# Two-operand arithmetic of the S5 and GLA stages on VectorE alone, table copies on ScalarE, other task lengths in the order

## The chip, the cores and the metric

One core of a Trainium2 chip runs the whole program. TensorE (PE in the rows) multiplies matrices, VectorE (DVE) and ScalarE (ACT) work on elements, GpSimd (POOL) does too and issues some DMAs, SyncE (SP) issues most DMAs. The metric is the device time of one execution in microseconds (us); lower is better.

## The reference

One layer of a hybrid model on 640 tokens (512 latent, 128 context) of 1024 features, in float32. What is computed, cut to what matters here:

```python
h = rms_norm(x) * (1 + scale1) + shift1
q, k, v, r, glr, u, ga, gb = split(h @ w_in)
# GLA: 4 heads, 2 directions, chunks of 64 tokens
log_a = log_sigmoid(glr @ w_gate_up + b_gate) / 16
cum = cumsum(log_a, within a chunk)
q_dec, k_in, k_out = q*exp(cum), k*exp(-cum), k*exp(total-cum)
o = tril(q_dec @ k_in.T) @ v + q_dec @ state;  state = exp(total)*state + k_out.T @ v
o_gla = rms_norm(o) * silu(r)
# S5: 32 groups of 16 channels, 64 complex states a group, 2 directions
lam_bar = exp(lam * exp(log_step)); b_bar = (lam_bar-1)/lam * b
s[t] = lam_bar * s[t-1] + b_bar @ u[t];  y = Re(c @ s) + d*u
o_s5 = gelu(y) * sigmoid(gelu(y) @ w_glu + b_glu)
merged = sigmoid(ga)*(o_gla @ w_proj_gla) + sigmoid(gb)*(o_s5 @ w_proj_s5)
x = x + gate1 * (merged @ w_out)
x = x + gate2 * (relu((rms_norm(x)*(1+scale2)+shift2) @ w_ff1)**2 @ w_ff2)
```

## The kernel before

**The main stream.** The weights come as slabs of 128x1024 through SyncE's queue (line 150). Each slab is split into two parts of lower precision: ScalarE rounds the high part `whi` (line 167), VectorE subtracts for the low part `wlo` (line 174). The features are split likewise into `hh` and `hl`, so that every product is three TensorE products of 320 or 512 columns (`whi`hh, `whi`hl, `wlo`hh). There are two buffers each of `whi` and `wlo`: a slab is split while the one before it is multiplied. The products come in units of one slab: u (4 units), k and q (4 each), v (8), then the S5 gate GLU, the low-rank gate, the S5 projection `ps`, the gates r and gb (8 units each), `gp` (the GLA projection, which merges), `wo`, and the two feed-forward products.

**The side work.** S5 and GLA run beside this stream. Each piece is a task: an engine, an estimated length, a function. The class `Sides` is a list scheduler that runs while the program is written: it counts up a planned time by the products that it has emitted, and emits a task between two products once the estimates say that its inputs are there. So the lengths decide at which place in every engine's list of instructions a task stands; on the chip each engine works through its own list in that order and waits by semaphore where an input isn't there yet. `sd.force()` at the end of v and at the end of gb emits all tasks that are left, with no products between them.

**S5's tasks**, for four sets q of eight channel groups (called group 0 to 3 below) and two directions d: `G` builds the input kernel from powers of lambda (two 128x1152 multiplications and an addition: `s5_g1` to `s5_g3`), `T` transposes it (line 844), `C` builds the output kernel in the same way (`s5_c1` to `s5_c3`), `K` multiplies both (32 products) and `P` stores the result to DRAM and reads it back as a Toeplitz matrix, `U` and `V` bring in u (which goes through DRAM too), `B` makes the rotation tables (`s5_tab`: six 128x256 operations and three copies), `R` rotates, scans and rotates back on VectorE (scans on lines 966 and 968), `Y` and `O` give the output, GELU on ScalarE follows. `C` of a group may not start before `Y` of the group before has read the old result, and `B` needs `R` of the group before. Before all of them stand constants that depend on lambda alone: `lam_p` on GpSimd makes the powers for the tables, `lt`, `lx`, `lq0` and `lq1` those for G and C.

**GLA's tasks**, for four heads: `z` (gate, logarithm, running sum, exponentials), `qk0` to `qk2` (decayed q and k), `kt` (transposes of k), `sm` and `st` (states), `sc` (scores), `fin`, `oa` to `oc` (outputs), `no` (norm), `og` (transposes and the gate r). A gate unit (r, gb) is followed by a logistic function in four steps on ScalarE and VectorE and a multiplication.

**The helpers.** `tt(o, a, b, op, e)` (line 207) is a two-operand operation on VectorE, or on GpSimd where the last argument is `G`; `mm` (line 219) is a product. Nearly all rows of the trace therefore have one of these two lines, and the tile names and shapes tell them apart. Names: `B`, `H` and `XB` are the working tiles, `aux` the single PSUM banks of the side work, `mm` the banks of the stream, `raw` the loaded slabs. In this version GpSimd has one of the two multiplications of each `G` and `C`, the six operations of every `B`, half of the lambda powers (`lq0`), `qk2` and the last multiplication after each r unit.

Of the kernel before, what the change touches and what calls it, by code (L numbers as in the profile page):

```python
# [29 lines left out]
class Sides:  # L30
    """Static list scheduler. The main stream of matrix products is emitted in order; the side work is a list of
    tasks with estimated lengths per engine, each emitted between the products when its inputs should be there."""
# [10 lines left out]
    def add(self, name, steps, after=(), banks=0, at=0.0, first=False, lazy=False):  # L43
        """a chain of steps (engine, length, function); the chain ends with the name given."""
        new = []
        for n, (eng, us, fn) in enumerate(steps):
            last = n == len(steps) - 1
            new.append((name if last else f"{name}.{n}", eng, us, fn, tuple(after), banks, at))
            after, banks, at = [f"{name}.{n}"], 0, 0.0
            if lazy:  # L50
                self.lazy.add(new[-1][0])
        if first:
            n = max((j + 1 for j, t in enumerate(self.todo) if t[0][:1] == "w" and name[0] == "w"), default=0)
            self.todo[n:n] = new
        else:
            self.todo += new
# [55 lines left out]
    def chain(self, name, wait=True):  # L112
        """emits what is left of a chain and lets the main stream wait for its end."""
        self.finish(*[t[0] for t in self.todo if t[0] == name or t[0].startswith(name + ".")])
        if wait:
            self.now["PE"] = max(self.now["PE"], self.end[name])

    def room(self, banks):
        """lets the side work go on until banks are free."""
        while 4 - len(self.held) < banks:  # L120
            self.run(next(t for t in self.todo if t[5] <= 4 - len(self.held) and all(a in self.end for a in t[4])))

    def force(self, name=None):
        """emits everything up to a task, whatever the estimates say."""
        while self.todo and (name is None or any(t[0] == name for t in self.todo)):
            self.run(self.todo[0])


class Weights:
    """Streams the weight slabs: DMA ahead, then an exact split into two float32r parts."""  # L130
# [24 lines left out]
    def ahead(self, w):  # L155
        """plans the splits of the main stream's slabs up to the w-th."""
# [24 lines left out]
    def first(self):  # L181
        """the first slab's raw data and the tiles of its parts, which the caller splits."""
        hi, lo = (self.pool.tile([128, 1024], F32R, tag=t, name=t, bufs=2) for t in ("whi", "wlo"))
        self.cut, self.parts[0], raw = 1, (hi, lo), self.raw.pop(0)
        self.sides.end["w0"] = 0.0
        self.top_up()
        return hi, lo, raw
# [14 lines left out]
def hybrid(tc, A, O):  # L202
# [19 lines left out]
    with contextlib.ExitStack() as ctx:  # L222
# [29 lines left out]
        # ---------------------------------------------------------------- first loads  # L252
# [66 lines left out]
        # ---------------------------------------------------------------- startup  # L319
# [33 lines left out]
        # ---- S5 constants that depend on lambda only, on the pair columns  # L353
        def sgt(o, a, s, b, op0, op1, tmp):
            """(a op0 s) op1 b on Pool, which has no single instruction for it."""
            ts(tmp, a, s, op0, e=G)
            tt(o, tmp, b, op1, G)
# [76 lines left out]
        def lam_5():  # L434
            # coefficient (lambda_bar - 1) / lambda
            ts(t2, LR, -1.0, ADD)
            tt(CR, t2, lre, MUL)
            tt(va, LI, lim, MUL)
            tt(CR, CR, va, ADD)
            tt(CR, CR, den, MUL)  # L440
# [8 lines left out]
        def lam_6():  # L449
            # ... times the conjugate of the phase of lambda^8  # L450
# [12 lines left out]
        def lam_p():  # L463
            # powers of the phase of lambda^8
# [26 lines left out]
        # stacked powers: X = [re; im] of lambda^k, Y = i * X, per group  # L491
# [47 lines left out]
        # ---- adaLN  # L539
# [5 lines left out]
        def mod_first(bank, j, i, a=None):  # L545
            """shift1 and scale1 of 256 features: even contraction tiles in the first two row groups, odd ones in the others."""
# [33 lines left out]
        # ---- position embedding and the first norm's statistics  # L580
# [41 lines left out]
        def warm(n):  # L622
            """keeps the tensor engine's clock up while the first data arrives."""
# [77 lines left out]
        def tok_unit(w, hi, lo, kts, banks, first, last, hooks={}, ahead=1, order=range(5)):  # L701
            """token-major: rows of 128 tokens times 512 columns, two contraction tiles."""
# [18 lines left out]
        def feat_part(ps, parts, hi, lo, first, n, nk=8, sub=0, lead=None):  # L721
            """feature-major: 128 features times n tokens."""
# [49 lines left out]
        # ---------------------------------------------------------------- S5  # L772
# [21 lines left out]
        S5 = {}  # L794
# [14 lines left out]
        def s5_g1(q, d):  # L809
            Bv, bb, kv = s5_views(q, d)  # L810
            tt(prod, bb(Bv[1]), kv(Q2, d), MUL, G)
# [10 lines left out]
        def s5_c1(q, d):  # L822
            Bv, bb, kv = s5_views(q, d)
            tt(prod, bb(Bv[3]), kv(YY, d), MUL, G)
# [59 lines left out]
        def s5_tab(q, d):  # L884
# [7 lines left out]
            tt(vr_, ar, br, MUL, G)  # L892
            tt(w, ai, bi, MUL, G)
            tt(vr_, vr_, w, SUB, G)
            tt(vi_, ar, bi, MUL, G)
            tt(w, ai, br, MUL, G)
            tt(vi_, vi_, w, ADD, G)
            for tab in (tabr, tabi):
                G.tensor_copy(tab[:, d, :, 64:80], tab[:, d, :, 48 * d:48 * d + 16])
            G.tensor_copy(rho_t[:, d], rho[:, cols][:, :, None].to_broadcast([128, 4, 81]))  # L900
# [35 lines left out]
        def s5_r1(q, d):  # L936
            """rotates the chunk inputs and sets the starting states."""
# [36 lines left out]
        def s5_r3(q, d, im):  # L974
            """rotates back and stacks [re; im] of each group."""
# [37 lines left out]
        def s5_f1():  # L1013
            # the final context states: wfin * u^16
# [20 lines left out]
        # ---------------------------------------------------------------- main stream  # L1035
# [3 lines left out]
        def add_gen(q):  # L1039
            p = q - 1  # L1040
            for d in range(2):
                last = [f"G{q}0", f"T{q}0"] if d else ([f"C{p}1", f"T{p}1", f"K{p}"] if q else [])
                sd.add(f"Gp{q}{d}", [("G", 2.1, L(s5_g1, q, d))], ["lq0"] + last)
                sd.add(f"Gq{q}{d}", [("V", 1.35, L(s5_g2, q, d))], ["lq0", "lq1"] + last)
                sd.add(f"G{q}{d}", [("V", 1.5, L(s5_g3, q, d))], [f"Gp{q}{d}", f"Gq{q}{d}"])
# [3 lines left out]
        def add_out(q):  # L1049
            p = q - 1  # L1050
            for d in range(2):
                sd.add(f"B{q}{d}", [("G", 6.1, L(s5_tab, q, d))], ["lamP"] + ([f"R{p}{d}"] if q else ["c11"]))
            for d in range(2):
                last = [f"C{q}0"] if d else [f"G{q}1"] + ([f"Y{p}0", f"Y{p}1", f"K{p}"] if q else ["c3", "lamD"])
                sd.add(f"Cp{q}{d}", [("G", 2.1, L(s5_c1, q, d))], last)
                sd.add(f"Cq{q}{d}", [("V", 1.3, L(s5_c2, q, d))], last)
                sd.add(f"C{q}{d}", [("V", 1.3, L(s5_c3, q, d))], [f"Cp{q}{d}", f"Cq{q}{d}"])
# [4 lines left out]
        def add_h(name, ks, steps, at):  # L1062
            """the modulation of h for the next features, while u is multiplied."""
# [42 lines left out]
        sd.add("lq0", [("G", 4.5, L(lam_q, 0, G))], ["lx"], lazy=True)  # L1106
# [38 lines left out]
        for q in range(4):  # L1145
# [3 lines left out]
            for d in range(2):  # L1149
                sd.add(f"V{q}{d}", [("PE", 1.3, L(s5_v, q, d))], [f"U{q}", f"T{q}{d}"] + ([f"R{q}0.0"] if d else []), 2)  # L1150
                sd.add(f"R{q}{d}", [("V", 2.5, L(s5_r1, q, d)), ("V", 1.6, L(s5_r2, q, d)),
                                    ("V", 1.7, L(s5_r3, q, d, 0)), ("V", 1.7, L(s5_r3, q, d, 1))], [f"V{q}{d}", f"B{q}{d}"])
# [60 lines left out]
        # ---------------------------------------------------------------- S5: GLU  # L1213
# [7 lines left out]
        def logistic(o, ps, copy=None):  # L1221
            """exp(min(x, 0) - ln(1 + exp(-|x|))), which needs one table only."""
# [19 lines left out]
        def follow(name, steps, after=()):  # L1242
            """what happens to a product, emitted while the next ones run."""
# [19 lines left out]
        # 32 features only: the weights' both parts lie side by side in the array, their sums follow below  # L1263
# [9 lines left out]
        # the gate's contraction of 32 holds all three parts of the split product: [hi; hi; lo] times [hi; lo; hi]  # L1273
# [88 lines left out]
        # ---------------------------------------------------------------- GLA  # L1362
# [18 lines left out]
        def gla_qk(h, d):  # L1381
# [17 lines left out]
            def qk2():  # L1399
                tt(blk(t1_), blk(t2_), bc(dm[d][1]), MUL, G)  # L1400
                tt(blk(q128[d]), blk(qd), bc(dm[d][0]), MUL, G)

            return [("V", 1.0, qk0), ("V", 1.5, qk1), ("G", 2.6, qk2)]
# [183 lines left out]
        for f in range(8):  # L1587
# [3 lines left out]
            follow(f"r{f}", logistic(x, ps, o) + [("G", 1.55, lambda o=o, x=x: tt(o, o, x, MUL, G))])  # L1591
# [5 lines left out]
        # ---------------------------------------------------------------- merge  # L1597
# [17 lines left out]
        def spread(t, row):  # L1615
            """a DRAM row of 512s on every partition."""
# [28 lines left out]
        # ---------------------------------------------------------------- output projection, residual  # L1645
# [29 lines left out]
        def res_rstd(t):  # L1675
            """the second half's sum of squares goes straight into the reciprocal root."""
# [9 lines left out]
        def add_res(name, bk, gt, tmps, release):  # L1686
            """residual and sums of squares of the first half of the features."""
# [87 lines left out]
        # ---------------------------------------------------------------- feed-forward  # L1775
# [83 lines left out]
        for t in range(5):  # L1859
            tl = slice(t * 128, (t + 1) * 128)  # L1860
            y, r = yo[:, t], rs5[:, t:t + 1]
            # the last tile's columns come in two halves, what is added to the second one last in a bank of its own
# [29 lines left out]
def layout(inp):  # L1892
    """Lays the inputs out for the program; no arithmetic on the data."""
# [121 lines left out]
```

## Time and profile before

| | us |
|---|---|
| median of three runs (1155.35 to 1156.99) | 1156.74 |
| span of the profiled execution | 1154.6 |
| TensorE busy | 1093.9 (95%) |
| VectorE busy | 659.1 (57%) |
| ScalarE busy | 424.5 (37%) |
| GpSimd busy | 271.4 (24%) |
| first k product to GLU (k, q, v beside S5) | 64.1 to 293.7 |
| GLU to the first product of the merge (GLA beside the gates) | 293.7 to 526.5 |
| merge, output projection, feed-forward, output | 526.5 to 1154.6 |

The profiled execution's own time is its span, 1154.6 us; the runs' median lies 2.1 us above it. Of the profile the following is to be read: the busy time and the granted clock by stretch, what TensorE waited for, and the timelines at the ends of the two middle stretches.

### The profile page before, as it was taken

What the parts mean: (1) busy time and instruction counts of PE and PEld (TensorE: products, weight loads), DVE (VectorE), ACT (ScalarE), POOL (GpSimd) and SP (SyncE); (2) the same over time, 40 slices, a digit from 0 to 9 for tenths busy, and PEclk for the clock granted to TensorE, in tenths of its full rate; (3) what the DMA queues carried; (4) which work ended last, traced back from release to release, by engine and by line L of the source; (5) the groups of instructions that cost most, each with busy time, mean ns of one, the idle gap of its engine ahead of it and who ended that gap; (6) DMA issues with size and microseconds to landing.
All of it is one profiled execution on the core that took longest, in us unless ns stands there. A gap on an engine that the chain in (4) does not pass through costs nothing. (4 is left out here: it accounts for less than half of the span.)

```text
span 1154.6 us, 17132 instructions
## 1 busy us (share of the span) xinstructions
PE 1093.9 (95%) x7055; PEld 982.2 (85%) x7055; DVE 659.1 (57%) x938; ACT 424.5 (37%) x650; POOL 271.4 (24%) x342
## 2 busy tenths in 40 slices
PE   9888798989999899999999999999999999999997
PEld 7676586667899798999999878999999988888886
DVE  6677987976577878954334477222222434345544
ACT  5222232132665476754222333222222323334334
POOL 7893655550020415110032022000000000000301
PEclk9998898989999999999999999999999999999999
DMA  9453434425321122123342601222222222222312
GB/s 381 157 174 120 149 108 153 138 77 173 131 74 55 47 65 65 50 107 128 93 145 73 222 34 56 75 79 82 76 73 74 74 74 73 85 80 91 110 37 91
DMA packets 42614, 119.77 MB, mean 104 GB/s; under 512 B 8204, under 2 KB 14876, under 8 KB 41512
## 3 DMA queue, kind: packets, MB, share of 16 engines
q1 hardware_dynamic: 39000, 107.81, 28.5%
q0 software_dynamic: 1520, 8.32, 1.9%
q10 hardware_dynamic: 2016, 2.56, 0.8%
q8 instruction: 55, 0.90, 0.3%
q14 instruction: 23, 0.19, 0.1%
HBM read 113.13 MB, written 5.54 MB: 103 GB/s over the span
## 5 line engine op out<-in xcount | busy, mean ns | idle before, releaser
L219 PE MATMUL mm<-H,whi 128*128 128x320 f32 (+2 forms) x1280 | 281.8, 309 | 0.0
L219 PEld LDWEIGHTS mm<-H,whi 128*128 128x128 f32 x1280 | 213.8, 188 | 0.1
L174 DVE TENSOR_TENSOR wlo<-raw,whi 128x1024 fp32r<-128x1024 f32 x121 | 162.9, 1347 | 69.9 <-ACT whi L167 65.4
L219 PE MATMUL mm<-H,wlo 128*128 128x320 f32 (+2 forms) x640 | 197.8, 309 | 0.0
L219 PE MATMUL mm<-hh,whi 128*128 128x320 f32 (+1 forms) x528 | 168.1, 321 | 1.8 <-DVE XB L216 1.2
L219 PE MATMUL mm<-hh,wlo 128*128 128x320 f32 x512 | 160.3, 313 | 4.8 <-DVE wlo L174 4.8
L219 PE MATMUL mm<-hl,whi 128*128 128x320 f32 (+1 forms) x528 | 164.0, 313 | 0.0
L167 ACT ACTIVATE whi<-raw 128x1024 fp32r<-128x1024 f32 x122 | 128.2, 1050 | 95.9 <-DMA raw<-in_W 70.9
L207 POOL TENSOR_TENSOR B<-B,XB 128x256 f32<-128x256 f32 (+5 forms) x68 | 89.2, 1328 | 215.5 <-DVE B L207 110.3
L219 PE MATMUL mm<-whi,B 128*128 128x512 f32 x416 | 138.5, 389 | 0.0
L207 DVE TENSOR_TENSOR B<-B,B 128x320 f32<-128x320 f32 (+9 forms) x124 | 99.7, 839 | 58.2 <-ACT B L1807 50.8
L219 PEld LDWEIGHTS mm<-H,wlo 128*128 128x128 f32 x640 | 120.2, 188 | 0.0
L207 DVE TENSOR_TENSOR B<-B 64x320 f32<-64x320 f32 (+4 forms) x116 | 69.6, 606 | 83.9 <-ACT B L744 74.6
L219 PEld LDWEIGHTS mm<-hh,whi 128*128 128x128 f32 (+1 forms) x528 | 100.3, 190 | 10.0 <-ACT H L744 4.2
L219 PEld LDWEIGHTS mm<-hh,wlo 128*128 128x128 f32 x512 | 98.1, 192 | 5.5 <-DVE wlo L174 5.5
L219 PEld LDWEIGHTS mm<-hl,whi 128*128 128x128 f32 (+1 forms) x528 | 100.4, 190 | 0.4
L219 PEld LDWEIGHTS mm<-whi,B 128*128 128x128 f32 x416 | 78.1, 188 | 16.2
L207 POOL TENSOR_TENSOR B<-B,free1k 128x512 f32<-128x512 f32 x4 | 5.2, 1288 | 358.6 <-DVE free1k L207 358.6
L219 PE MATMUL mm<-wlo,B 128*128 128x512 f32 x208 | 80.9, 389 | 0.0
L219 PE MATMUL aux<-whi,B 128*128 128x512 f32 x224 | 79.2, 389 | 0.0
L207 POOL TENSOR_TENSOR B<-B 128x32 f32<-128x32 f32 (+3 forms) x80 | 48.0, 610 | 23.9 <-DVE B L216 9.9
L744 ACT ACTIVATE B<-mm 128x640 f32<-128x640 f32 x24 | 16.9, 704 | 93.2 <-PE mm L219 88.9
(290 smaller groups left out, 1711.0 us busy)
## 6 DMA issues: line engine op xcount, KB each, us to landing
raw<-in_W SPq DMA_DIRECT2D x130, 512.0 KB, 3.5
raw<-in_WM SPq DMA_DIRECT2D x32, 512.0 KB, 4.6
H<-in_xT SPq DMA_DIRECT2D x4, 640.0 KB
B<-in_xt POOLq DMA_DIRECT2D x2, 1280.0 KB, 6.5
out_y<-yo SPq DMA_DIRECT2D x10, 256.0 KB, 2.0
H<-in_WM SPq DMA_DIRECT2D x2, 1024.0 KB, 7.5
B<-in_WM SPq DMA_DIRECT2D x2, 1024.0 KB
H<-in_WM SPq DMA_DIRECT2D x4, 512.0 KB, 10.3
```

Of the source, the lines that this page charges most:

```text
L167: self.nc.scalar.activation(box["hi"], self.raw[p], AF.Copy)
L174: self.nc.vector.tensor_tensor(lo, raw, hi.bitcast(F32), SUB)
L207: (e or V).tensor_tensor(o, a, b, op)
L219: PE.matmul(o, l, r, start=start, stop=stop, skip_group_check=True)
L744: S.activation(two(o), ps, func, **kw)
```

## The change

The two-operand operations that GpSimd had in the S5 and GLA stages go to VectorE: 8 + 8 of 128x1152 (`s5_g1`, `s5_c1`), 48 of 128x256 (`s5_tab`), 6 of 128x256 (`lq0`), 16 of 128x640 (`qk2`) and 8 of 128x640 (after the r units). The three copies at the end of `s5_tab` become ScalarE copies in a function of their own. The task lengths of G, C, B, R, `lq0`, `qk` and the r multiplication are set anew, and the split tasks `Gp`, `Gq`, `Cp`, `Cq` become chains. Comments go too, so line numbers shift by up to 3.

```diff
         def s5_g1(q, d):
             Bv, bb, kv = s5_views(q, d)
-            tt(prod, bb(Bv[1]), kv(Q2, d), MUL, G)
+            tt(prod, bb(Bv[1]), kv(Q2, d), MUL)
...
         def s5_c1(q, d):
-            tt(prod, bb(Bv[3]), kv(YY, d), MUL, G)
+            tt(prod, bb(Bv[3]), kv(YY, d), MUL)
...
-            tt(vr_, ar, br, MUL, G)
-            tt(w, ai, bi, MUL, G)
+            tt(vr_, ar, br, MUL)
+            tt(w, ai, bi, MUL)
...
+        def s5_tab2(q, d):
+            cols = slice(d * 16 + 4 * q, d * 16 + 4 * q + 4)
             for tab in (tabr, tabi):
-                G.tensor_copy(tab[:, d, :, 64:80], tab[:, d, :, 48 * d:48 * d + 16])
-            G.tensor_copy(rho_t[:, d], rho[:, cols][:, :, None].to_broadcast([128, 4, 81]))
+                S.activation(tab[:, d, :, 64:80], tab[:, d, :, 48 * d:48 * d + 16], AF.Copy)
+            S.activation(rho_t[:, d], rho[:, cols][:, :, None].to_broadcast([128, 4, 81]), AF.Copy)
...
-                sd.add(f"Gp{q}{d}", [("G", 2.1, L(s5_g1, q, d))], ["lq0"] + last)
-                sd.add(f"Gq{q}{d}", [("V", 1.35, L(s5_g2, q, d))], ["lq0", "lq1"] + last)
-                sd.add(f"G{q}{d}", [("V", 1.5, L(s5_g3, q, d))], [f"Gp{q}{d}", f"Gq{q}{d}"])
+                sd.add(f"G{q}{d}", [("V", 1.4, L(s5_g1, q, d)), ("V", 1.4, L(s5_g2, q, d)), ("V", 1.7, L(s5_g3, q, d))], ["lq0", "lq1"] + last)
...
-                sd.add(f"B{q}{d}", [("G", 6.1, L(s5_tab, q, d))], ["lamP"] + ([f"R{p}{d}"] if q else ["c11"]))
+                sd.add(f"B{q}{d}", [("V", 2.6, L(s5_tab, q, d)), ("S", 1.0, L(s5_tab2, q, d))], ["lamP"] + ([f"R{p}{d}"] if q else ["c11"]))
...
             def qk2():
-                tt(blk(t1_), blk(t2_), bc(dm[d][1]), MUL, G)
-                tt(blk(q128[d]), blk(qd), bc(dm[d][0]), MUL, G)
+                tt(blk(t1_), blk(t2_), bc(dm[d][1]), MUL)
+                tt(blk(q128[d]), blk(qd), bc(dm[d][0]), MUL)
```

The order of instructions moves with it, at three places above all.

**Where u ends.** VectorE before: the lambda powers (`B_107`, `B_83`), then the two copies that empty PSUM banks of u (line 1134).

```order
L207 TENSOR_TENSOR B_83<-B_107,B_83 128x64
L207 TENSOR_TENSOR B_107<-B_107,B_83 128x64 x2
L207 TENSOR_TENSOR B_83<-B_107,B_83 128x64
L207 TENSOR_TENSOR B_107<-B_107,B_83 128x64
L1134 COPY H_783<-aux_313 128x512
L1134 COPY H_783<-mm 128x512
L207 TENSOR_TENSOR B_107<-B_107,B_83 128x128
```

No table operation stands here; GpSimd has them. VectorE after: the last three of the twelve table operations of group 0 (`B_90` from the powers `B_73` and `XB`), then the two copies (line 1133), then more lambda work and the next slab's split.

```order
L207 TENSOR_TENSOR B_90<-B_73,XB 128x4x64
L207 TENSOR_TENSOR B_90<-B_73,XB 128x256
L207 TENSOR_TENSOR B_90<-B_90 128x4x64
L1133 COPY H_744<-aux_313 128x512
L1133 COPY H_744<-mm 128x512
L207 TENSOR_TENSOR B_106<-B_106 128x32 x3
L174 TENSOR_TENSOR wlo<-raw,whi 128x1024
```

The tables of group 0 have come in ahead of u's copies; the lambda powers have gone behind them. 

ScalarE before, at the same place (line 510 takes over transposes of lambda powers, line 1132 empties three banks of u):

```order
L167 ACTIVATE whi<-raw 128x1024
L510 ACTIVATE B_83<-aux_740 128x384
L510 ACTIVATE B_83<-aux_749 128x384
L1132 ACTIVATE H_783<-mm 128x512 x3
L167 ACTIVATE whi<-raw 128x1024
```

Nothing of the tables stands here. ScalarE after (lines 902 and 903 are the table copies, 1131 the banks of u):

```order
L167 ACTIVATE whi<-raw 128x1024
L902 ACTIVATE B_90<-B_90 128x4x16 x2
L903 ACTIVATE XB<-XB 128x324
L1131 ACTIVATE H_744<-mm 128x512 x3
L167 ACTIVATE whi<-raw 128x1024
```

The three copies for the first direction's tables have come in ahead of u's three banks.

**The end of v.** TensorE before: the last products of v, the adaLN product (32x512), and the GLU's first products.

```order
L219 MATMUL mm<-whi,hh 128x512
L219 MATMUL mm<-wlo,hh 128x512
L219 MATMUL mm<-whi,hl 128x512
L219 MATMUL aux_1838<-raw,sc 32x512 x4
L219 MATMUL mm<-B_2570,whi 128x320
L219 MATMUL mm<-B_2571,whi 128x320
```

S5 is over here before the last products. TensorE after: behind the same products and the adaLN product now stand K of group 2 (32x128 x16) and the transposes of group 3 (line 844), and behind them, down to the GLU, Y and O of group 2, K, U, V, Y and O of group 3.

```order
L219 MATMUL mm<-whi,hh 128x512
L219 MATMUL mm<-wlo,hh 128x512
L219 MATMUL mm<-whi,hl 128x512
L219 MATMUL aux_1646<-raw,sc 32x512 x4
L219 MATMUL aux_2281<-B_81,B_107 32x128 x16
L844 MATMUL aux_2331<-par,B_91 128x128 x4
L844 MATMUL aux_2336<-par,B_91 128x128 x4
L844 MATMUL aux_2347<-par,B_91 128x128 x4
```

What lay among the v products has moved behind them.

VectorE after, at the same place: the last slab split, one adaLN sum, then the addition of K of group 2 (`aux_2281`), which the rows above produce:

```order
L207 TENSOR_TENSOR B_106<-B_106,B_90 128x4x80 x2
L174 TENSOR_TENSOR wlo<-raw,whi 128x1024
L207 TENSOR_TENSOR mrow<-mrow,aux_1646 128x512
L207 TENSOR_TENSOR B_82<-B_82,aux_2281 128x32
L207 TENSOR_TENSOR B_91<-B_81 128x32
L207 TENSOR_TENSOR B_82<-B_82,B_91 128x32
L207 TENSOR_TENSOR B_90<-B_106,B_90 128x320 x2
```

All that VectorE has left of S5 stands behind this addition: one rotation's rest, G, B and C of group 3, and its two rotations.

**The end of gb.** TensorE before: the last transposes of head 3 (lines 1537 and 1538) lie among the gate products; 75 rows of them follow before the merge.

```order
L219 MATMUL mm<-hh,wlo 128x320
L1537 MATMUL aux_4634<-par,H_797 128x128 x4
L1538 MATMUL aux_4636<-par,H_797 128x128
L1537 MATMUL aux_4635<-par,H_797 128x128 x4
L1538 MATMUL aux_4636<-par,H_797 128x128
L219 MATMUL mm<-hh,whi 128x320
L219 MATMUL mm<-hl,whi 128x320
```

Head 3 ends among the gate products here. TensorE after: the last gate products are followed by head 3's transposes of k (line 1446) and its states.

```order
L219 MATMUL mm<-hh,whi 128x320
L219 MATMUL mm<-hl,whi 128x320
L219 MATMUL mm<-hh,wlo 128x320
L1446 MATMUL aux_4620<-par,B_2791 128x128 x4
L1446 MATMUL aux_4626<-par,B_2792 128x128 x4
L219 MATMUL aux_4632<-H_758,XB 128x256 x2
```

Before, `kt` and the states of head 3 lay several units ahead of this. The last transposes of head 3, after, and what stands directly behind them, the merge's first products:

```order
L219 MATMUL aux_4709<-B_2797,B_2796 128x256 x2
L1536 MATMUL aux_4731<-par,H_758 128x128 x4
L1537 MATMUL aux_4733<-par,H_758 128x128
L1536 MATMUL aux_4732<-par,H_758 128x128 x4
L1537 MATMUL aux_4733<-par,H_758 128x128
L219 MATMUL mm<-hh,whi 128x320
L219 MATMUL mm<-hl,whi 128x320
```

Head 3 from `kt` on has moved from among the gate products to behind them.

## Rows read from the trace of the kernel before

**Rows 1.** Stretches: length; PE, PEld, DVE, ACT, POOL busy us (instructions); clock; DMA share; GB/s.

```profile
64.13:293.69 229.56, 195.40 (x1459) 157.48 (x1457) 185.38 (x271) 60.27 (x100) 116.67 (x122) 0.91 0.43 136
293.69:526.50 232.81, 223.20 (x1593) 212.15 (x1590) 170.07 (x257) 143.94 (x251) 47.13 (x35) 0.99 0.24 78
526.50:1154.60 628.10, 616.15 (x3569) 568.01 (x3567) 261.12 (x294) 193.60 (x256) 54.51 (x35) 1.00 0.27 86
```

**Rows 2.** TensorE's longest waits: waiting line, releaser, us in total, times, longest.

```profile
PE aux L844 <- DVE B L207: 11.2, 2, 7.0
```

**Rows 3.** Timeline, both engines: start, duration, engine, line, operation, out<-in, [idle before <-releaser].

```profile
92.02 2.29 POOL L207 TENSOR_TENSOR B<-B,B 128x1152 f32<-128x1152 f32 x1 [1.47 <-DVE B L207]
...
92.12 3.27 DVE L174 TENSOR_TENSOR wlo<-raw,whi 128x1024 fp32r<-128x1024 f32 x1
...
95.31 1.35 DVE L207 TENSOR_TENSOR B<-B,B 128x1152 f32<-128x1152 f32 x1
```

**Rows 4.** Groups by shape (busy us, mean ns | idle); then one timeline row.

```profile
L207 POOL TENSOR_TENSOR B<-B,XB 128x256 f32<-128x256 f32 x32 | 35.5, 1129 | 27.6 <-DVE B L207 27.6
...
L207 DVE TENSOR_TENSOR B<-B,B 128x256 f32<-128x256 f32 x12 | 9.8, 862 | 0.1
...
47.79 0.41 DVE L207 TENSOR_TENSOR B<-B,aux 128x256 f32<-128x256 f32 x1
```

**Rows 5.** Timeline where u ends: GpSimd, then ScalarE, then TensorE.

```profile
68.27 0.88 POOL L207 TENSOR_TENSOR B<-B,XB 128x256 f32<-128x256 f32 x1
...
62.29 1.09 ACT L1132 ACTIVATE H<-mm 128x512 f32<-128x512 f32 x2 [0.38 <-PE mm L219]
...
64.13 0.30 PE L219 MATMUL mm<-hh,whi 128*128 128x320 f32 x1
```

**Rows 6.** Timeline of TensorE after a wait of 3.12 us.

```profile
76.52 0.98 PE L913 MATMUL aux<-par,B 80*128 80x80 f32 x8 [3.12 <-ACT B L907]
...
79.51 0.47 PE L219 MATMUL mm<-hh,wlo 128*128 128x320 f32 x1
...
80.48 0.30 PE L219 MATMUL mm<-hh,whi 128*128 128x320 f32 x1
```

**Rows 7.** Timeline of S5's last group: VectorE, then TensorE.

```profile
261.93 1.68 DVE L207 TENSOR_TENSOR B<-aux,B 128x320 f32<-128x320 f32 x4
...
270.17 1.56 DVE L968 TENSOR_TENSOR_SCAN B<-XB,B 128x324 f32<-128x324 f32 x2
...
272.05 0.89 DVE L207 TENSOR_TENSOR B<-B,B 128x320 f32<-128x320 f32 x2
...
272.97 0.99 DVE L207 TENSOR_TENSOR B<-B 64x320 f32<-64x320 f32 x2
...
265.18 1.08 PE L219 MATMUL aux<-B,B 128*32 128x128 f32 x32
...
280.37 0.42 PE L219 MATMUL aux<-B,XA 128*80 128x128 f32 x2 [1.49 <-DMA B<-kd]
...
285.57 0.48 PE L219 MATMUL mm<-whi,hh 128*128 128x512 f32 x1
...
292.69 1.07 PE L219 MATMUL aux<-raw,sc 128*32 128x512 f32 x8
```

**Rows 8.** Timeline of GLA's end: TensorE, VectorE, ScalarE, VectorE.

```profile
494.84 2.48 PE L219 MATMUL aux<-B 128*64 128x64 f32 x60
...
503.83 1.02 PE L219 MATMUL aux<-H,B 128*128 128x256 f32 x4
...
508.57 1.03 PE L219 MATMUL aux<-B,B 128*128 128x256 f32 x4
...
512.41 1.41 DVE L211 TENSOR_SCALAR H<-H,XB 128x256 f32<-128x256 f32 x5
...
526.57 0.70 ACT L1224 ACTIVATE XB<-mm 128x640 f32<-128x640 f32 x1 [2.37 <-PE mm L219]
...
530.47 0.83 DVE L207 TENSOR_TENSOR B<-B,XB 128x640 f32<-128x640 f32 x1 [0.80 <-ACT XB L1238]
```

More of the change, by code (lines that the diff above doesn't have):

```diff
@@ L891, in s5_tab @@
             w = tmpp.rearrange("p q (a b) -> p q a b", a=8)
-            tt(vr_, ar, br, MUL, G)
-            tt(w, ai, bi, MUL, G)
[L894 to L897, printed above, removed]
+            tt(vr_, ar, br, MUL)
+            tt(w, ai, bi, MUL)
+            tt(vr_, vr_, w, SUB)
+            tt(vi_, ar, bi, MUL)
+            tt(w, ai, br, MUL)
+            tt(vi_, vi_, w, ADD)
+        def s5_tab2(q, d):
+            cols = slice(d * 16 + 4 * q, d * 16 + 4 * q + 4)
             for tab in (tabr, tabi):
-                G.tensor_copy(tab[:, d, :, 64:80], tab[:, d, :, 48 * d:48 * d + 16])
-            G.tensor_copy(rho_t[:, d], rho[:, cols][:, :, None].to_broadcast([128, 4, 81]))
+                S.activation(tab[:, d, :, 64:80], tab[:, d, :, 48 * d:48 * d + 16], AF.Copy)
+            S.activation(rho_t[:, d], rho[:, cols][:, :, None].to_broadcast([128, 4, 81]), AF.Copy)
             G.memset(rho_t[:, d, :, 64:81:16], 0.0)
@@ L1051, in add_out @@
             for d in range(2):
-                sd.add(f"B{q}{d}", [("G", 6.1, L(s5_tab, q, d))], ["lamP"] + ([f"R{p}{d}"] if q else ["c11"]))
+                sd.add(f"B{q}{d}", [("V", 2.6, L(s5_tab, q, d)), ("S", 1.0, L(s5_tab2, q, d))], ["lamP"] + ([f"R{p}{d}"] if q else ["c11"]))
             for d in range(2):
                 last = [f"C{q}0"] if d else [f"G{q}1"] + ([f"Y{p}0", f"Y{p}1", f"K{p}"] if q else ["c3", "lamD"])
-                sd.add(f"Cp{q}{d}", [("G", 2.1, L(s5_c1, q, d))], last)
-                sd.add(f"Cq{q}{d}", [("V", 1.3, L(s5_c2, q, d))], last)
-                sd.add(f"C{q}{d}", [("V", 1.3, L(s5_c3, q, d))], [f"Cp{q}{d}", f"Cq{q}{d}"])
+                sd.add(f"C{q}{d}", [("V", 1.4, L(s5_c1, q, d)), ("V", 1.4, L(s5_c2, q, d)), ("V", 1.4, L(s5_c3, q, d))], last)
             sd.add(f"K{q}", [("PE", 1.3, L(s5_k1, q)), ("S", 0.6, L(s5_k2, q)), ("V", 0.4, L(s5_k3, q))],
@@ L1105, in hybrid @@
         sd.add("lx", [("V", 0.9, L(lam_x, 2, 1, 4)), ("V", 1.2, L(lam_x, 3, 2, 6)), ("V", 2.3, L(lam_x, 5, 4, 8))], ["lt"], lazy=True)
-        sd.add("lq0", [("G", 4.5, L(lam_q, 0, G))], ["lx"], lazy=True)
+        sd.add("lq0", [("V", 2.3, L(lam_q, 0))], ["lx"], lazy=True)
         sd.add("lq1", [("V", 2.3, L(lam_q, 4))], ["lx"], lazy=True)
@@ L1150, in hybrid @@
                 sd.add(f"V{q}{d}", [("PE", 1.3, L(s5_v, q, d))], [f"U{q}", f"T{q}{d}"] + ([f"R{q}0.0"] if d else []), 2)
-                sd.add(f"R{q}{d}", [("V", 2.5, L(s5_r1, q, d)), ("V", 1.6, L(s5_r2, q, d)),
-                                    ("V", 1.7, L(s5_r3, q, d, 0)), ("V", 1.7, L(s5_r3, q, d, 1))], [f"V{q}{d}", f"B{q}{d}"])
+                sd.add(f"R{q}{d}", [("V", 2.9, L(s5_r1, q, d)), ("V", 2.6, L(s5_r2, q, d)),
+                                    ("V", 1.95, L(s5_r3, q, d, 0)), ("V", 1.95, L(s5_r3, q, d, 1))], [f"V{q}{d}", f"B{q}{d}"])
             if q < 3:
@@ L1399, in qk2 @@
             def qk2():
-                tt(blk(t1_), blk(t2_), bc(dm[d][1]), MUL, G)
-                tt(blk(q128[d]), blk(qd), bc(dm[d][0]), MUL, G)
-            return [("V", 1.0, qk0), ("V", 1.5, qk1), ("G", 2.6, qk2)]
+                tt(blk(t1_), blk(t2_), bc(dm[d][1]), MUL)
+                tt(blk(q128[d]), blk(qd), bc(dm[d][0]), MUL)
+            return [("V", 1.3, qk0), ("V", 1.65, qk1), ("V", 1.65, qk2)]
         t5 = lambda v: v[:, 0:320].rearrange("p (t i) -> p t i", t=5)
@@ L1590, in hybrid @@
             x = sr[(f + 2) // 4][:, (f + 2) % 4 * T:((f + 2) % 4 + 1) * T] if f in (1, 3, 5) else ogt
-            follow(f"r{f}", logistic(x, ps, o) + [("G", 1.55, lambda o=o, x=x: tt(o, o, x, MUL, G))])
+            follow(f"r{f}", logistic(x, ps, o) + [("V", 0.82, lambda o=o, x=x: tt(o, o, x, MUL))])
         for f in range(8):
```

## The prediction

> **What bounds the kernel now.** I read four things in order: the busy time by stretch, TensorE's list of waits, the timeline where VectorE and GpSimd meet, and the order of instructions. By stretch [rows 1], TensorE works 195.4 of the 229.6 us from the first k product to the GLU, so 34.2 us are idle; its mean granted clock there is 0.91. Since its products run at one of two levels, full or half, 0.09 of 195.4 = 17.6 us more go to the lower one. In the GLA stretch the same sums give 9.6 and 2.2 us. From 526.5 us on it is busy 98% and nothing that the change touches lies there. So the change has 52 + 12 us to win in two stretches, and TensorE's order decides the rest: its products are one list, and a wait anywhere in it stops all that stand behind.
>
> The longest wait of S5 is TensorE's transposes (line 844) for VectorE, 11.2 us in two [rows 2]. Why VectorE is late shows in [rows 3]: its split of a weight slab starts 0.10 us after a GpSimd multiplication, takes 3.27 us, and ends when 1.2 us after the GpSimd one has ended. The two lie one behind the other, not beside each other.
>
> That is what the Trainium skill ("SBUF — State Buffer", section "SBUF: two separate sides") says: VectorE's second port pair is shared with GpSimd as an exclusive lock, so whoever starts first blocks the other for a whole instruction. The row agrees: 2.2 us of blocking before about 1.2 us of work. By that rule the change takes away 2.29 us of blocking and puts 1.35 in its place; I take it as the rival "faster" below.
>
> **Part by part: prices.** A 128x1152 multiplication costs 2.29 us on GpSimd and 1.35 on VectorE [rows 3]. A table operation of 128x256 costs 1.13 on GpSimd; on VectorE 0.41 undisturbed and 0.86 as a mean of twelve that ran beside GpSimd [rows 4]. I take 0.41, since after the change GpSimd is empty there, and keep 0.86 for the range (the new ones read strided, broadcast operands, which no row shows). A 128x640 multiplication on VectorE is 0.83 [rows 8]. Per S5 group VectorE gets four 128x1152 (5.4 us) and twelve table operations (4.9 us) more. What it had before: eight 128x1152 for G and C (10.8 us), two rotations R, and small sums and copies (about 4, an estimate). One R is 1.68 + 0.89 to rotate, about 2.2 for the scans with the small copies around them, and twice 0.89 + 0.99 to rotate back [rows 7]: 8.5 us. So VectorE alone has 32 + 10 = 42 us a group; before, its 32 and GpSimd's 4 x 2.29 + 12 x 1.13 = 23 lay one behind the other to the extent that they met, at most 55. Inside the stream this is a gain, and I take nearly all the idle time there as gone. The three small copies that go to ScalarE (0.3 to 0.6 us each, an estimate from the ScalarE copies of [rows 5]) lie beside other work, with one exception that follows.
>
> **Early stall.** The tables of group 0 need the powers that GpSimd computes until 68.3 us [rows 5]. Before, GpSimd itself waited for them, and nobody stood behind. Now the twelve table operations stand on VectorE ahead of the two copies that empty u's banks, and two table copies and a third one stand on ScalarE ahead of its three. u's last product ends at about 62.2, 1.9 us before 64.13 (the lambda transposes, 1.9 us by an estimate from the timeline of [rows 5], go behind the first products of k). VectorE: 68.3 + 6 x 0.41 = 70.8. ScalarE: three copies, 1.2, then two of u's, 1.09 [rows 5]: 73.1. The first k product starts there instead of at 64.13. Behind it are the 1.9 us of the transposes and half-clock products: after the 3.12 us wait in [rows 6] products stood at 0.47 us until 80.3 and at 0.30 from 80.48 on, which cost about 1.9 us. Together 9.0 + 1.9 + 1.9 = 12.8 us later.
>
> **The stream.** At full clock and without idle, the stretch from k to the GLU is 195.4 - 17.6 = 177.8 us of TensorE work. Of that the new order puts about 19 us behind the last v product (see below). 158.8 + 1.9 + 1.9 = 162.6 remain, 3 us for U of group 0, which waits again for u's way through DRAM as in [rows 6]: the stream ends at 73.1 + 165.6 = 238.7; with all stalls gone, and the transposes inside other waits, at 235. I take 237.
>
> **The bare tail of S5.** Here the order decides against the change. In the second piece of the order TensorE's last 512-column v product is followed by K of group 2, T of group 3, Y and O of group 2, and K, U, V, Y, O of group 3, with no main product between them. Before, those products lay between the last two v units, and S5 was over while v still ran (Y ends at 285.57, the stream at 292.69 + 1.07 [rows 7]). VectorE can't run ahead of it either: directly behind the split of the last slab it adds up K of group 2, which is a product behind the stream's end. From then VectorE has: one back rotation of R20 1.9, scan and back rotations of R21 6.0, G 4.2 + 4.2, tables 4.9, C 8.1, two rotations 17.1, small ones 1.6: 48 us. Between them lie waits that nothing covers: K of group 2 and its copy 2.4; C waits for Y of group 2, 1.5; K, U and V of group 3 (1.08 [rows 7], 0.98 [rows 6], about 1.3, with the copies between) 6; Y 5.2 [rows 7], at half clock up to 7; O, GELU and the split of y 5. Together 68 to 71; I take 69. The store and reload of K (before, Y waited for it 14 us behind K's end, with 1.49 of idle time at the end of that [rows 7]) takes less than the two R and stays hidden behind them; on SyncE's queue only slab loads stand ahead of it, and GpSimd's queue gets shorter. GLU starts at 237 + 69 = 306, against 293.7, with 1.9 us for the low clock: **+14.2 us**.
>
> **The bare tail of GLA.** The third piece of the order shows the same: before, 75 more main products stand behind head 3's last transposes; now the whole of head 3 from kt on stands behind the last gate product, and the first of the merge behind it. On VectorE qk of head 3 stands behind the last gate's multiplication, which comes 4.7 us after the product ends [rows 8]. Then: qk 2 x 5 x 0.81 = 8.0; kt and its copy 1.3; sm 2.4; sc 2.5 [rows 8] with its copies 1.9; oa to oc 5.8 [rows 8] after fin 0.8; squares, root and scaling 1.6 + 0.6 + 2.2 (of it 1.41 in [rows 8]); og 1.3. That is 33, with the queues' gaps and half clock 34.5. In it are about 14 us of TensorE work (5.8, 2.5, 16 products at the pace of oa to oc, 18 transposes). The stretch: 232.8 - 9.6 - 2.2 - 14 + 1.5 (waits that stay) + 34.5 + 1.9 (low clock behind it) = 244.9: **+12.1 us**.
>
> **Sum.** 1154.6 + 14.2 + 12.1 = 1180.9 us of span. The profiled execution's span stands 2.1 us under the median of 1156.74; so 1183.
>
> **The rivals.** *Faster.* The lock is all that matters: 52 + 12 us of idle and low clock vanish, less the early 12.8, so about 1105 at best. For it speak [rows 2, 3]. It would need the last group's chain and the last head's to end inside their streams. The price turns at the tail of S5: with GLA's +12 the case is even when that tail is 69 - 26 = 43 us, and VectorE's own work in it is 48 before any wait. The order of before has no such tail; the one after does, whatever the engines' speeds. Chance 0.03. *Same,* for instance because the shorter tasks happen to balance the tails: 0.02; that the change doesn't do what it says is out, since the order has 115 fewer GpSimd rows. *Lighter:* the powers come earlier, as VectorE leaves GpSimd alone there, 3 us; products behind stalls lose no clock, 4; tails 4 + 3 shorter: 1169. Chance 0.13. *Heavier:* table operations at 0.86, so 12 x 0.45 = 5 in the tail, 3 early and, where VectorE then is late in the stream, up to 10: 1197. Chance 0.12. The forecast has 0.70.
>
> The Trainium skill ("Perfetto Trace Analysis", section "Optimizing GPSIMD Operations") advises to use other engines than GpSimd where one can. The prices above agree, 1.35 to 2.29; the sum by that rule alone would be the rival "faster".
>
> **How the numbers follow.** Forecast 1183 with its own range 1175 to 1191; with the lighter and heavier cases 1168 to 1197, which leaves out half of "heavier", and "same" and "faster". A change under 0.2% (2.3 us) can't be told from none here. Faster 0.03, same 0.02, slower 0.95.
>
> **What would show it.** Early: VectorE's first table operation at about 68 us after a wait for GpSimd, and k's first product at 73. In the stream: slab splits of 1.2 us throughout, transposes without a wait. S5's tail: from about 237 to 306 TensorE mostly idle, VectorE nearly full for 48 us, with the clock low. GLA's: some 20 us of idle time after the last gate product, then the merge. If the tails are there but under 50 and 25 us, my latencies are too long; if TensorE still waits for VectorE inside the stream, the price of the table operations is wrong; if the main products lie among the tail's tasks, I read the order wrongly and the prediction falls.

## The result and the profile after

The kernel after takes 1195.2 us (median of four runs, 1194.64 to 1196.81), the kernel before beside it 1156.87: a ratio of 1.0337, 95% interval 1.0322 to 1.0351. That is 38.3 us slower, where the prediction had 1183 (26 slower) and a range of 1168 to 1197. The sign and the range hold; the size fell short by 12 us.

The busy time of the kernel after by stretch, cut where its own stages end (the columns as in [rows 1]):

```profile
0.00:72.38 72.38, 55.98 (x410) 41.86 (x411) 44.55 (x112) 26.40 (x46) 57.06 (x164) 0.94 0.59 225
72.38:249.62 177.24, 167.75 (x1224) 135.24 (x1228) 134.59 (x243) 49.23 (x86) 0.62 (x7) 0.98 0.53 165
249.62:318.56 68.94, 28.62 (x269) 25.31 (x261) 50.83 (x105) 14.17 (x35) 0.84 (x4) 0.68 0.14 43
318.56:564.60 246.04, 227.21 (x1588) 214.71 (x1589) 169.83 (x279) 148.46 (x255) 5.41 (x14) 0.95 0.21 66
564.60:1193.90 629.30, 618.25 (x3570) 569.86 (x3568) 262.45 (x296) 192.00 (x253) 55.06 (x36) 0.99 0.28 87
```

The first row ends where k's first product starts, 8.25 us later than before [rows 5]. The second is k, q and v with S5 beside them: TensorE busy 95%, granted clock 0.98, GpSimd empty. The third is S5's tail: 68.94 us in which TensorE works 28.62 us, and VectorE 50.83; the mean clock of the stretch is 0.68. The fourth is GLA, 246.04 us against 232.81 [rows 1]. The last has hardly moved, 629.3 against 628.1.

What TensorE waited for (in total, times, longest; as in [rows 2]):

```profile
PE aux L844 <- DVE B L207: 18.1, 3, 13.5
PE aux L219 <- DVE B L207: 16.4, 6, 8.1
PE aux L1446 <- DVE B L207: 13.7, 2, 10.9
PE mm L219 <- ACT H L1131: 11.5, 1, 11.5
PE aux L219 <- DMA B<-kd: 8.3, 2, 4.3
```

Before, next to the transposes of [rows 2], the slab splits (`wlo`) led the list with 13.2 us together:

```profile
PE aux L219 <- DVE wlo L174: 8.4, 3, 5.5
PE mm L219 <- DVE wlo L174: 4.8, 2, 2.7
```

After, they are gone from its head. In their place stand waits of tails: transposes of group 3, the outputs of groups 2 and 3, head 3's transposes of k (line 1446), and one for u's copies (line 1131).

The timeline of the early wait, one row of VectorE, one of ScalarE, one of TensorE, then a product of TensorE 4 us later:

```profile
66.42 0.82 DVE L207 TENSOR_TENSOR B<-B,XB 128x256 f32<-128x256 f32 x1 [9.29 <-POOL B L207]
...
71.26 1.06 ACT L1131 ACTIVATE H<-mm 128x512 f32<-128x512 f32 x2
...
72.38 0.64 PE L219 MATMUL mm<-hh,whi 128*128 128x320 f32 x1 [11.54 <-ACT H L1131]
...
76.55 0.47 PE L219 MATMUL mm<-hh,whi 128*128 128x320 f32 x1
```

VectorE stands 9.29 us at its first table operation, waiting for GpSimd's powers. ScalarE empties u's first two banks only at 71.26 (before, at 62.29 [rows 5]), and TensorE starts k at 72.38, with products of 0.47 us until 77. While it waited, its granted clock had fallen to the lower level, 0.50 from 64 to 68 us, a stretch in which it has no instruction (its row below, columns as above):

```profile
64.00:68.00 4.00, 0.00 (x0) 0.00 (x0) 0.82 (x1) 0.00 (x0) 3.76 (x10) 0.50 0.00 0
```

So the mean clock of a stretch counts its idle time too.

S5's tail on TensorE, from K of group 2 to the GLU's first product:

```profile
249.62 1.06 PE L219 MATMUL aux<-B,B 128*32 128x128 f32 x32
...
264.17 1.94 PE L844 MATMUL aux<-par,B 128*128 128x128 f32 x8 [13.49 <-DVE B L207]
...
283.50 1.08 PE L219 MATMUL aux<-B,B 128*32 128x128 f32 x16 [3.32 <-DVE B L207]
...
297.31 0.69 PE L219 MATMUL aux<-B,XA 128*80 128x128 f32 x2 [4.27 <-DMA B<-kd]
...
307.94 0.71 PE L219 MATMUL aux<-B,B 128*80 128x128 f32 x2 [8.07 <-DVE B L207]
...
318.56 0.41 PE L219 MATMUL mm<-B,whi 128*128 128x320 f32 x1 [1.55 <-ACT B L1169]
```

Each of these waits is for one step of the same chain: G, C, the reload of K, the second rotation, the split of y. No main product stands between them. GLA's end has the same form; first the last gate's multiplication on VectorE, then TensorE's two longest waits:

```profile
535.14 0.83 DVE L207 TENSOR_TENSOR B<-B,XB 128x640 f32<-128x640 f32 x1 [0.80 <-ACT XB L1237]
...
539.27 1.09 PE L1446 MATMUL aux<-par,B 128*128 128x128 f32 x4 [10.88 <-DVE B L207]
...
562.38 1.17 PE L1536 MATMUL aux<-par,H 128*128 128x128 f32 x4 [3.31 <-DVE H L211]
```

TensorE stops 10.88 us ahead of 539.27, so at 528.4, and is back in main products at 564.6: 36 us, the tail that the prediction put at 34.5.

### The profile page after: what moved, and what is told of

The parts are those of the page before. It is cut to its first block, busy times and chain, and to the rows that moved or that the text cites. A ratio compares the mean times of both kernels' runs of the same rounds, so it can differ in the third digit from the quotient of the medians.

```text
span 1193.9 us, 17076 instructions
## 1 busy us (share of the span) xinstructions
PE 1097.8 (92%) x7055; PEld 987.0 (83%) x7055; DVE 662.2 (55%) x1032; ACT 430.3 (36%) x674; POOL 119.0 (10%) x224
## 5 line engine op out<-in xcount | busy, mean ns | idle before, releaser
L174 DVE TENSOR_TENSOR wlo<-raw,whi 128x1024 fp32r<-128x1024 f32 x121 | 151.8, 1255 | 90.5 <-ACT whi L167 85.3
L207 DVE TENSOR_TENSOR B<-B 64x320 f32<-64x320 f32 (+5 forms) x134 | 72.5, 546 | 83.1 <-ACT B L744 74.6
L219 PE MATMUL aux<-B,B 128*32 128x128 f32 (+2 forms) x320 | 44.5, 317 | 13.8 <-DVE B L207 13.8
L207 DVE TENSOR_TENSOR B<-B,XB 128x256 f32<-128x256 f32 (+3 forms) x73 | 43.1, 621 | 18.9 <-POOL B L207 10.2
L219 PEld LDWEIGHTS aux<-whi,B 128*128 128x128 f32 x224 | 42.0, 188 | 8.7
```

What stands on the lines that cost most here:

```text
L174: self.nc.vector.tensor_tensor(lo, raw, hi.bitcast(F32), SUB)
L207: (e or V).tensor_tensor(o, a, b, op)
L219: PE.matmul(o, l, r, start=start, stop=stop, skip_group_check=True)
```

## The experiments

Two things are in this change: operations move to VectorE and ScalarE, and the new lengths move tasks in every engine's list. **Theory A**: the places cost the time, and the move itself gains. **Theory B**: the move costs it, because VectorE has too much work for one engine. Later came **theory C**: the places of before were laid out for two engines, so VectorE falls behind when all the work stands there.

### e1: tables of group 0 behind u's copies

```diff
-  sd.add(f"B{q}{d}", ..., ["lamP"] + ([f"R{p}{d}"] if q else ["c11"]))
+  sd.add(f"B{q}{d}", ..., ["lamP"] + ([f"R{p}{d}"] if q else ["c11", "ue"]))
...
-  sd.end["u"] = sd.now["PE"] + 7.0
+  sd.end["u"], sd.end["ue"] = sd.now["PE"] + 7.0, sd.now["PE"]
```

> The kernel after, with one change: the rotation tables of group 0 may not be emitted until the copies that empty u's banks are. Theory A (the order of instructions costs the time: an early wait of some 12 us, and two tails without main products): k's first product comes at about 64 us instead of 72.4 after an 11.5 us wait, both tails stay, 1183 us. Theory B (VectorE is now the engine with too much work, whatever the order): VectorE's work is the same, so the time given back early is lost again in the stream, 1192 to 1196 us.

1187.6 us, a ratio of 1.027 (1.0254 to 1.0285): 7.6 us less than the kernel after, not 12, and far more than none. The edit also moves the lambda transposes back ahead of k, which therefore starts at 66.79 and not at 64; so it is not a pure test of the wait. e6 is.

### e2: the order of after, the engines of before

```diff
-  tt(prod, bb(Bv[1]), kv(Q2, d), MUL)
+  tt(prod, bb(Bv[1]), kv(Q2, d), MUL, G)
...
-  tt(blk(t1_), blk(t2_), bc(dm[d][1]), MUL)
+  tt(blk(t1_), blk(t2_), bc(dm[d][1]), MUL, G)
```

and so on for every operation that had moved; task lengths and TensorE's list as in the kernel after.

> The order of the kernel after, word for word, but with every operation that was moved put back on GpSimd, the table copies too. Theory A: the tails are there without any moved operation, and hold slower ones: no early wait, S5's tail 75 to 85 us, GLA's about 38; stalls in the stream as before or more: 1185 to 1215 us. Theory B: with the work back on two engines the time is near that of the kernel before, 1155 to 1165 us.

1196.54 us, a ratio of 1.0348 (1.033 to 1.0365). The slowdown is there in full without a single moved operation, and without the early wait (k starts at 61.09). Its tail on TensorE, from K of group 2 to the GLU:

```profile
243.27 1.06 PE L219 MATMUL aux<-B,B 128*32 128x128 f32 x32
...
256.56 1.94 PE L844 MATMUL aux<-par,B 128*128 128x128 f32 x8 [12.24 <-DVE B L207]
...
316.63 0.41 PE L219 MATMUL mm<-B,whi 128*128 128x320 f32 x1 [1.60 <-ACT B L1169]
```

73.4 us, against 68.9 in the kernel after: the same tail with slower operations in it. Theory B falls here.

### e3: the engines of after in lengths of before, tables of group 0 behind u's copies

```diff
   (the kernel before)
-  tt(vr_, ar, br, MUL, G)
+  tt(vr_, ar, br, MUL)
...
-  sd.add(f"B{q}{d}", [("G", 6.1, ...)], ["lamP"] + ([f"R{p}{d}"] if q else ["c11"]))
+  sd.add(f"B{q}{d}", [("G", 6.1, ...)], ["lamP"] + ([f"R{p}{d}"] if q else ["c11", "ue"]))
```

> The reverse: all operations moved to VectorE and ScalarE as in the kernel after, but the task lengths and so the places of the kernel before; only the tables of group 0 are kept behind u's copies. No tails in the order. Theory A: S5 ends inside v's products, head 3 inside gb's; the waits that came from GpSimd shrink from 34 to 20 us or less in S5 and from 10 to 5 in GLA: 1135 to 1157 us. Theory B: VectorE has 42 us of work a group in the place of 32, TensorE waits inside the stream, 1175 to 1200 us.

1174.15 us (1.0149, 1.0134 to 1.0164), which neither theory had. Its timeline shows why it decides nothing: keeping the tables behind u's copies moved tasks again, and Y of group 3 now stood behind the last v product, waiting for its reloaded K.

```profile
300.30 0.69 PE L219 MATMUL aux<-B,XA 128*80 128x128 f32 x2 [11.09 <-DMA B<-kd]
```

A tail had come back through the edit itself. In e5 TensorE's list was therefore held equal row by row.

### e4 and e11: the two halves

```diff
   e4 (the kernel before)
-  return [("V", 1.0, qk0), ("V", 1.5, qk1), ("G", 2.6, qk2)]
+  return [("V", 1.3, qk0), ("V", 1.65, qk1), ("V", 1.65, qk2)]
...
-  [("G", 1.55, lambda o=o, x=x: tt(o, o, x, MUL, G))]
+  [("V", 0.82, lambda o=o, x=x: tt(o, o, x, MUL))]
```

e11 is the kernel after with these lines, and the engine of `qk2`, as before.

> The kernel before with the GLA half of the change alone (qk2 and the r multiplications on VectorE, their task lengths). S5 is that of before. Theory A: GLA's tail alone, 12 to 14 us more: 1169 to 1171 us, with TensorE idle some 20 us behind the last gate product. Theory B: VectorE has 20 us more work in a stretch of 233 us where it is busy 170, which it can take: 1155 to 1160 us.

> The kernel after with GLA put back as it was before (engines and lengths): the S5 half of the change. If the two halves add up: 1157 + 38 - 12 = 1183 us, with S5's tail of 69 us and no tail behind the last gate product. If the late start lets GLA hide something: under 1180.

e4: 1168.94 us (1.0103, 1.0088 to 1.0118), e11: 1183.89 us (1.0231, 1.021 to 1.0253). GLA's half costs 12 us, S5's 27; their sum is 39, against the 38 of the whole. In e4 the wait behind the last gate product is that of the kernel after:

```profile
512.56 1.09 PE L1447 MATMUL aux<-par,B 128*128 128x128 f32 x4 [11.04 <-DVE B L207]
```

### e6: the kernel after, tables of group 0 back on GpSimd

```diff
-  tt(vr_, ar, br, MUL)
+  tt(vr_, ar, br, MUL, None if q else G)
...
-  S.activation(rho_t[:, d], ..., AF.Copy)
+  x = (rho_t[:, d], ...)
+  S.activation(*x, AF.Copy) if q else G.tensor_copy(*x)
```

> The kernel after with its own order on TensorE, row by row, except that the tables of group 0 and their copies are on GpSimd again. This takes the early wait away and nothing else. Theory A: k's first product 8 us earlier, no half-clock products behind it, 9 to 13 us less than the kernel after: 1182 to 1186 us; both tails as they were. If the early wait was hidden by later waits: 1192 to 1196 us.

1189.79 us (1183.9 to 1190.5; ratio 1.0288, 1.0261 to 1.0315): 5.4 less than the kernel after. k starts at 63.67, 8.7 us earlier, but K of group 2 at 242.51, only 7.1 earlier, and the GLU at 312.82, 5.7 earlier. Of the 8.7 us, 1.6 go before K of group 2, where waits come up that the early wait had covered, 1.4 in S5's tail and 0.4 behind it. One of them, for a slab split:

```profile
86.18 0.63 PE L219 MATMUL mm<-hh,wlo 128*128 128x320 f32 x1 [3.03 <-DVE wlo L174]
```

### e5, e9, e10: the engines moved, TensorE's list as before

In all three TensorE's list is that of the kernel before, row by row; lengths and labels stay, only the engine argument of operations changes. e5 moves all (the tables of group 0 excepted), e9 the multiplications alone, e10 the tables of groups 1 to 3 alone.

```diff
   e5, e9
-  tt(prod, bb(Bv[1]), kv(Q2, d), MUL, G)
+  tt(prod, bb(Bv[1]), kv(Q2, d), MUL)
...
   e5, e10
-  tt(vr_, ar, br, MUL, G)
+  tt(vr_, ar, br, MUL, None if q else G)
```

> All operations moved to VectorE and ScalarE as in the kernel after, but TensorE's list is that of the kernel before, row by row; the only other difference is that the tables of group 0 stay on GpSimd, so that nobody waits early for the lambda powers. Theory A (order alone decides; the engines themselves gain): TensorE's waits for VectorE shrink in S5, 1135 to 1157 us. Theory C (the order of before counts on two engines: VectorE's list now holds 10 us more a group than it was laid out for, so slab splits come late in v and k): 1162 to 1178 us, with waits for wlo and whi inside the stream.

> TensorE's list as in the kernel before; to VectorE go the multiplications alone (128x1152 of G and C, 128x640 of GLA, half of the lambda powers), the tables stay on GpSimd. If the gain of the run with all of it moved (1143 us) comes from the long multiplications that block slab splits and scans for 2.3 us a time: 1143 to 1148 us. If it comes from the tables: 1152 to 1157 us.

> The counterpart: TensorE's list as in the kernel before; only the tables of groups 1 to 3 with their copies go to VectorE and ScalarE, all multiplications stay on GpSimd. If the gain comes from the multiplications: 1152 to 1158 us. If from the tables (36 operations of 1.13 us, each of which blocks VectorE when they meet): 1143 to 1150 us.

e5: 1143.09 us (0.9892, 0.9874 to 0.991). e9: 1139.87 us (1135.39 to 1144.84; 0.9853, 0.9817 to 0.9888), which beats both kernels. e10: 1160.39 us (1.003, 1.0015 to 1.0046). In e9's profiled execution, the fastest of its four, the GLU starts at 276.63, 17 us earlier than before; the whole is 21 us shorter there, so most of the gain is S5's. So the move gains 13 us in the old places. By the medians the multiplications alone gain some 17 us and the tables alone cost 4; the intervals of e5 and e9 overlap. Theory C doesn't hold for e5. The group of slab splits between k's start and the GLU (count | busy us, mean ns | idle before), first the kernel before, then e9, then e10:

```profile
L174 DVE TENSOR_TENSOR wlo<-raw,whi 128x1024 fp32r<-128x1024 f32 x16 | 28.8, 1802 | 12.2 <-ACT whi L167 12.0
```

```profile
L174 DVE TENSOR_TENSOR wlo<-raw,whi 128x1024 fp32r<-128x1024 f32 x16 | 21.0, 1312 | 13.2 <-ACT whi L167 13.0
```

```profile
L174 DVE TENSOR_TENSOR wlo<-raw,whi 128x1024 fp32r<-128x1024 f32 x16 | 26.0, 1624 | 15.3 <-ACT whi L167 15.0
```

Before, a split takes 1.80 us on average. With the multiplications off GpSimd it takes 1.31, near the 1.23 of a split in the kernel after, where GpSimd has hardly any work (at 249.26); with the multiplications on GpSimd and the tables off it, 1.62. TensorE's waits of e9, then of e10:

```profile
PE aux L844 <- DVE B L207: 7.2, 2, 5.0
PE mm L219 <- DVE wlo L174: 4.6, 3, 2.6
```

```profile
PE aux L844 <- DVE B L207: 13.1, 2, 9.1
PE aux L219 <- DVE wlo L174: 7.1, 3, 6.1
PE mm L219 <- DVE wlo L174: 6.0, 2, 5.4
```

Before, these waits were 11.2 us for the transposes and 13.2 for the splits. Where one 2.29 us operation on GpSimd becomes 1.35 on VectorE, they fall; where 1.13 becomes about 0.5, they don't.

### e7 and e8: lengths that pull the work back into the stream

```diff
-  ("V", 1.4, L(s5_g1, q, d))
+  ("V", 0.98, L(s5_g1, q, d))
```

All VectorE lengths of G, C, B and R times 0.7 (e7) or 0.6 (e8), tables of group 0 on GpSimd, GLA as before.

> S5 as in the kernel after (VectorE), the tables of group 0 on GpSimd, GLA as in the kernel before, and all VectorE lengths of the S5 tasks G, C, B, R times 0.7. In TensorE's list Y of group 3 now ends with the last v product, so S5 has no tail but O and GELU. Theory A: the stretch from k to the GLU falls from 229.6 to 200 to 220 us, 1125 to 1150 us in all. Theory C: VectorE's work, 187 us of it, is packed closer than it can be done; waits inside the stream take the place of the tail, 1155 to 1175 us.

> As the run before, with the lengths times 0.6: Y of group 3 stands 87 products ahead of the end of v. Theory A: 1125 to 1150 us, within 5 us of the run before. Theory C: tasks stand still earlier than VectorE reaches them, 1160 to 1185 us, slower than the run before.

e7: 1155.27 us (1.0, 0.9985 to 1.0015), e8: 1164.31 us (1.0079, 1.0064 to 1.0094). The tail leaves the list, and e7 lies 29 us under e11 (some 5 of them for the early wait), but it gets no further than the kernel before. Its waits for slab splits are 12.8 us, about those of before (13.2); what has grown is the wait of Y for its reloaded K (1.5 us before), the longest of them in group 3:

```profile
PE aux L219 <- DMA B<-kd: 10.7, 3, 7.1
```

In e8 the waits for slab splits grow to 21.3 us:

```profile
PE mm L219 <- DVE wlo L174: 11.9, 3, 6.3
PE aux L219 <- DVE wlo L174: 9.4, 2, 8.0
```

The 8.0 in rows: `whi` of that slab is ready at 210.39, but tasks of S5 stand ahead of its split on VectorE until 217.89.

```profile
209.33 1.06 ACT L167 ACTIVATE whi<-raw 128x1024 fp32r<-128x1024 f32 x1 [12.95 <-DMA raw<-in_W]
...
217.89 1.23 DVE L174 TENSOR_TENSOR wlo<-raw,whi 128x1024 fp32r<-128x1024 f32 x1
```

For e8 theory C is right; for e7 it is not shown, since its splits wait no longer than before. So the lengths of the kernel after make a tail, and at 0.6 of them tasks stand ahead of splits.

## Why the prediction was right, and where it was off

The two orders and the two sets of engines, in us (the tables of group 0 on GpSimd in the lower right two):

| | engines of before | engines of after |
|---|---|---|
| order of before | 1156.9 | 1143.1 (e5) |
| order of after | 1196.5 (e2) | 1189.8 (e6); 1195.2 with the early wait |

- **What decides: the order.** Right. It costs 40 us with the old engines, 47 with the new ones; the move alone gains 13 in the old order and 7 in the new one, where much of it lies in tails.
- **Early stall.** The place was right: k at 72.38, forecast 73.1. Its price was not: the sum took 12.8 us, of which 1.9 were the transposes, whose place e6 keeps. Of the other 10.9, taking the wait away (e6) gives back 5.4. The step that failed is that the delay was carried to the end in full; later waits, like the 3.03 us in e6, were covered by it.
- **The stream.** This is the term that was mis-sized: K of group 2 was forecast at 237 and came at 249.62, 12.6 us later, which is the whole miss. From k's start on that is 177.24 against 163.9. In rows: 9.5 us are idle (177.24 - 167.75), where I had chosen 237 with about 1 us left of the 34; the largest is Y of group 0 for its reloaded K:

```profile
158.71 0.45 PE L219 MATMUL aux<-B,XA 128*80 128x128 f32 x2 [4.01 <-DMA B<-kd]
```

  The rest is the clock. I took the clock loss of before as 0.09 of the busy time, but the 0.91 counts idle time as well. Cut into pieces of half a microsecond, each with its own busy time and clock, the stretch from k to the GLU had lost 14.1 us to the lower clock before, and not 17.6 (these sums are estimates). So its full-clock work was 195.4 - 14.1 = 181.3 us, and not 177.8; the kernel after, taken the same way, has 181.4 without the transposes. And the low clock itself took 4.3 us of the stream, where I had 1.9. The 13.3 us are then 8.2 of idle time, 2.4 of low clock and 2.7 of work that was left out.
- **S5's tail.** Right, 68.94 against 69, and for the reasons given; that it fits so closely is luck, since two small errors cancel. VectorE is busy 50.83 us in it against 48, with the table operations at about 0.5 (two of 0.55 and one of 0.42), where I took 0.41, and not at 0.86; the waits that nothing covers are 18.1 us against 20 to 22. One step was off without changing the sum: the reload of K did not stay hidden, Y waited 4.27 us for it; but behind that it waited for the second rotation at 307.94 all the same.
- **GLA's tail.** Right: e4 alone costs 11.9 us by the medians, forecast 12.1; the tail was 36 us against 34.5.
- **The rival "faster"** did not come about, as its condition said: the tails stand whatever the engines' speeds. Its mechanism is real, though, and e5 and e9 show its size once the tails are away: 13 to 17 us, not the 50 that I had priced. Idle time stays even without GpSimd's multiplications: 24.5 us from k to the GLU in e9, against 34.2 before. The Trainium skill ("SBUF — State Buffer", section "SBUF: two separate sides") has the port pair that VectorE and GpSimd share as an exclusive lock, held for a whole instruction. e9 and e10 agree with it: a split takes 1.62 us where GpSimd multiplies, and 1.31 where it doesn't.
- **The sum.** Early start -0.7, stream +13.3, S5's tail 0, GLA with the low clock behind both tails -0.8, the rest of the kernel +1.2: 13.0 us between the forecast span of 1180.9 and 1193.9.
- **The range.** 1195.2 lies 2 us under its upper end, near the rival "heavier", but that it does so is not that rival's merit: the table operations took about 0.5 us and not 0.86, and in the stream TensorE waited 3.8 us for VectorE and not up to 10.
- **Slips in the working.** The split in [rows 3] ends 1.08 us after the GpSimd operation, not 1.2. The stream's lower bound is 73.1 + 162.6 - 1.9 = 233.8 and not 235. The terms of "heavier" add up to 1201; 1197 takes 6 of the 10 us for the stream. None of them moves the forecast itself by more than 1 us.

What stays open: why the tables cost a few us on VectorE in the old order (e10 is 3.7 slower than before, 1.5 to 4.6 parts in a thousand). The waits for splits and transposes in it are about as long as before (26.2 us against 24.4), and which of the added operations sets them was not tried. Open too is why the planner's lengths put these tails into the order, since S5's lengths were only changed together, by one factor.

## What to carry to other kernels

When a change touches the numbers from which a static order is made, read the order first: what stands behind the last product of a stage has no cover, and its price is the whole chain, 69 and 36 us here, whatever a single operation gains. To judge an engine move, hold the critical engine's list equal and change the engine argument alone; here that turned a 3.4% loss into a 1.1 to 1.5% gain. Lengths near the measured times (1.4 for a multiplication of 1.35 us) still gave the order with the tails: lengths have to be judged by where the last task lands.

## What the runs showed of the hardware

Table operations of 128x256 whose operands are broadcast take 0.55 us on VectorE, in-place ones of the same size 0.42; the forecast had one price of 0.41 for both. The two kinds differ in more than the broadcast, and which of it costs the 0.13 us was not tried. The timeline of VectorE in the kernel after, two of the former and one of the latter:

```profile
70.62 1.09 DVE L207 TENSOR_TENSOR B<-B,XB 128x256 f32<-128x256 f32 x2
71.75 0.42 DVE L207 TENSOR_TENSOR B<-B 128x256 f32<-128x256 f32 x1
```

Taking only the multiplications off GpSimd (e9, 1139.87) was not slower than emptying it (e5, 1143.09; their intervals overlap).
